# The opening of the first feed-forward layer: smaller first chunks, halved adaLN columns, modulation from PSUM

## The chip, the core and the metric

The kernel runs on one core of one Trainium2 chip. Time is device time in microseconds (us); each kernel is run several times and the median is given. TensorE (PE) multiplies, VectorE (DVE), ScalarE (ACT) and GpSimd (POOL) work on elements, SyncE (SP) issues the DMAs. Each engine works through its own queue in order and waits on semaphores that others raise.

## The reference

One Conformer-like block over 256 tokens of width 2048, with adaLN: nine vectors of 2048 (shift, scale, gate for three parts) come from `silu(c) @ w_ada + b_ada`.

```
def modulate(h, shift, scale):
    return h * (1 + scale[:, None, :]) + shift[:, None, :]
def swiglu(h, w_gu, w_down):
    gu = jnp.einsum('bsd,df->bsf', h, w_gu)
    g, u = jnp.split(gu, 2, axis=-1)
    return jnp.einsum('bsf,fd->bsd', jax.nn.silu(g) * u, w_down)
...
ada = jnp.einsum('bd,de->be', c_act, w_ada[l]) + b_ada[l]
sh1, sc1, g1, shm, scm, gm, sh2, sc2, g2 = jnp.split(ada, N_MOD, axis=-1)
h = modulate(rms_norm(x, ffn1_norm[l]), sh1, sc1)
x = x + FFN_RESIDUAL_WEIGHT * g1[:, None, :] * swiglu(h, ffn1_w_gu[l], ffn1_w_down[l])
h = modulate(rms_norm(x, mix_norm[l]), shm, scm)
x = x + gm[:, None, :] * hybrid_mixer(h, ...)
h = modulate(rms_norm(x, ffn2_norm[l]), sh2, sc2)
x = x + FFN_RESIDUAL_WEIGHT * g2[:, None, :] * swiglu(h, ffn2_w_gu[l], ffn2_w_down[l])
```

The width of the feed-forward layers is 5632; everything is float32.

## The kernel before

Activations stay on the chip; weights stream through once, mostly in tiles of 1 MB: four row tiles of 128 rows by 512 columns. Each tile is split in two parts: ACT rounds it (line 222, a CAST from `raw` to `whi`), DVE takes the exact remainder (line 224, `wlo`). The activations are split in the same way. A product is three passes on PE (lines 232 to 234): high by high, high by low, low by high, for each row tile and each of two tiles of 128 tokens. So a row tile has six matrix instructions, called products here. The token-tile accumulators of a chunk are in PSUM; ACT copies them out (line 345).

An adaLN column of 128 values comes from a tile of `w_ada` of 1 MB: DVE multiplies it by `silu(c)`, which stands on every partition, and sums along the row (line 152). Two columns, scale and shift, modulate one row tile of the activations (128 channels).

The first feed-forward layer has 22 chunks of 256 columns of gate and 256 of up. At its start only few adaLN columns are there, so stage A takes just the first row tiles of a chunk: `EXT` gives 1 for the first three chunks, 2 for three, 3 for five, and 4 for the rest. The rows left out come later: a second stage, A2, takes eight chunks (`n_a2`) through their first rest and second piece, then the chunks are finished one by one. The modulation of the first block of 512 channels is made in tiles: for each of the two token tiles DVE scales and shifts out of PSUM (line 293), ACT rounds (295), DVE subtracts (296).

The order is not written by hand engine by engine: the program is written as one sequence and a tile framework puts it into the engines' queues, by its own estimate of when things are ready. `issue_after` holds a DMA back in that order until another has been issued. Buffers are pools: four raw weight buffers (`raw`), four of `whi` and of `wlo`, 32 blocks of 4 KB per partition (`blk`), six accumulators. A DMA into a pool waits until the buffer's last reader is done. Loads run three tiles ahead (`AHEAD`) of the products.

Of the kernel before, what the change touches and what calls it, by code (L numbers as in the profile page):

```python
# [16 lines left out]
F32 = mybir.dt.float32  # L17
# [30 lines left out]
# columns of the packed small parameters  # L48
# [3 lines left out]
def _cols():  # L52
    pos = 0
    for name, n in (("bada", 144), ("ident", P), ("n1", 16), ("nm", 16), ("n2", 16), ("convw", 8 * CK),
                    ("convb", 8), ("lng", 8), ("lnb", 8), ("subln", 1), ("qn", DH), ("kn", DH), ("lam", 4 * DH),
                    ("inv", 32), ("mask", P)):
        _COLS[name] = (pos, n)
        pos += n
    return pos
# [6 lines left out]
def block_kernel(ctx: ExitStack, tc: tile.TileContext, x_in, c_in, pos_in, w_ada, small, w_gu1, w_dn1,  # L66
# [3 lines left out]
    blkp = ctx.enter_context(tc.tile_pool(name="blkp", bufs=32))  # L70
# [30 lines left out]
    # ---------------------------------------------------------------- constants  # L101
    c_bc = const.tile([P, D], F32, name="c_bc")
    c_row = [blk([1, 1024]) for _ in range(2)]
    ones_r = tmp([1, P])
    nc.gpsimd.memset(ones_r, 1.0)
    for i in range(2):
        nc.sync.dma_start(out=c_row[i], in_=c_in[:, i * 1024:(i + 1) * 1024])
        for j in range(2):
            pc = acc_tile()
            nc.tensor.matmul(pc, ones_r, c_row[i][:, j * 512:(j + 1) * 512], start=True, stop=True)  # L110
            o = (2 * i + j) * 512
            nc.scalar.activation(out=c_bc[:, o:o + 512], in_=pc, func=AF.Silu)
    cst = const.tile([P, NCOLS], F32, name="cst")
    pos_i = const.tile([P, NT], I32, name="pos_i")

# [4 lines left out]
    ident = col("ident")  # L120
    identb = const.tile([P, P], BF16, name="identb")
    maskb = const.tile([P, P], BF16, name="maskb")
    half = const.tile([P, 8], F32, name="half")
    nc.gpsimd.memset(half, -0.5)

    def rstd_of(ss, n, count, eps):
# [16 lines left out]
    # ---------------------------------------------------------------- adaLN projections  # L143
    ada_cols = {}

    def ada(j):
        g = j // 8
        if j % 8 == 0:
            ada_cols[g] = const.tile([P, 8], F32, name=f"ada{g}")
# [8 lines left out]
    ada_next = [0]  # L158
# [18 lines left out]
    def modulation(base, k, norm):  # L177
        """Scale and shift columns of the 128-channel tile k."""
# [9 lines left out]

    def gate(base, scale):
        """The gate's 2048 values on every partition, as four [P, 512] views (through DRAM)."""  # L190
# [37 lines left out]

    def mm3(acc, a, w, start, stop):
# [6 lines left out]
    def mm_tile(accs, w, act, k0, start, stop, ts=(0, 1), ks=(0, 4)):  # L236
        """One weight tile (row tiles ks of the four from k0) into the accumulators of the token tiles."""
# [8 lines left out]
    # ---------------------------------------------------------------- residual stream  # L246
    x = []
# [9 lines left out]
    class Norm:  # L257
        """RMS norm and modulation of the residual stream into split, transposed activations."""
# [13 lines left out]
        def begin(self, kb, t, vec):  # L272
            """Normalised and transposed tokens, still without modulation."""
# [14 lines left out]
        def tile(self, st_, kb, t, j):  # L288
            """One 128-channel tile, modulated and split."""
            tp, hf = st_  # L290
            G, SH = modulation(self.base, 4 * kb + j, self.norm)
            hi = self.hh[kb][:, j, t * P:(t + 1) * P]
# [32 lines left out]
    # ---------------------------------------------------------------- FFN  # L325
    HOLD = 3        # weight tiles held across a change of the activations
    HOLD_DN = 2     # and at the end of a down projection

    def ffn(st, w_gu, w_dn, gate_base, ada_a, ada_b, nxt, n_a2, n_a3):
        """nxt: the norm that follows (None after the last layer).  # L330

        Stage A takes the first row tiles of every chunk.  Then n_a2 chunks get their second piece (the
        last n_a3 of them the third too) ahead of the rest, so that the adaLN columns have time to come.
        """
# [12 lines left out]
        def pieces(after=None):  # L347
            # the last activations take the place that the first leave after stage A
# [6 lines left out]
        begun = 4 * bool(st.done)       # row tiles whose activations are there  # L355
        ext = [4] * NCH                 # row tiles of a chunk in stage A
        if not st.done:
            # the first modulations arrive one 128-channel tile at a time
            sts = [st.begin(0, t, True) for t in range(NT)]
            ws = []  # L360
            for c in range(NCH + AHEAD):
                if c < NCH:
# [583 lines left out]
```

## Time and profile before

| | |
|---|---|
| three runs | 1874.54, 1870.46, 1874.64 us |
| median | 1874.54 us |
| span of the profiled execution, first to last instruction | 1872.4 us |
| the profiled execution's own time | not given apart from its span; the median of the runs is 2.1 us above the span |
| mean granted TensorE clock | 0.995 of full |
| PE, DVE, ACT busy in the span | 98%, 77%, 48% |

A row of the timeline gives an instruction, or several alike that follow each other, with its start, its length, and in brackets how long its engine stood idle before it and what ended that. A matrix instruction is drawn with a modelled end and overlaps the next one, so the distance of two starts is the rate. The clock is given as a share of full: 1.00 is 2.4 GHz and 0.50 is 1.2 GHz.

### The profile page before, as it was taken

What the parts mean: (1) busy time and instruction counts of PE and PEld (TensorE: products, weight loads), DVE (VectorE), ACT (ScalarE), POOL (GpSimd) and SP (SyncE); (2) the same over time, 40 slices, a digit from 0 to 9 for tenths busy, and PEclk for the clock granted to TensorE, in tenths of its full rate; (3) what the DMA queues carried; (4) which work ended last, traced back from release to release, by engine and by line L of the source; (5) the groups of instructions that cost most, each with busy time, mean ns of one, the idle gap of its engine ahead of it and who ended that gap; (6) DMA issues with size and microseconds to landing.
All of it is one profiled execution on the core that took longest, in us unless ns stands there. A gap on an engine that the chain in (4) does not pass through costs nothing.

```text
span 1872.4 us, 21954 instructions
## 1 busy us (share of the span) xinstructions
PE 1838.1 (98%) x8295; PEld 1510.8 (81%) x8295; DVE 1439.3 (77%) x1921; ACT 905.5 (48%) x1363; POOL 30.9 (2%) x34
## 2 busy tenths in 40 slices
PE   6999999999999999999999999999999999999999
PEld 3788888888888888778877788888888888888887
DVE  6779889988888777789999688775877755544443
ACT  4654354444444434454876555654444444433332
POOL 0000000000000000000110100000000000000000
PEclk9999999999999999999999899999999999999999
DMA  8888978888898888646343696895777755555552
GB/s 312 341 315 328 364 272 327 330 326 329 317 345 330 335 340 333 226 170 210 137 158 138 241 344 257 328 355 202 274 285 272 275 197 180 190 215 205 201 212 79
DMA packets 72141, 495.92 MB, mean 265 GB/s; under 512 B 8114, under 2 KB 8290, under 8 KB 14052
## 3 DMA queue, kind: packets, MB, share of 16 engines
q1 hardware_dynamic: 72036, 494.53, 71.5%
q8 instruction: 65, 1.06, 0.2%
q14 instruction: 40, 0.33, 0.1%
HBM read 492.37 MB, written 2.12 MB: 264 GB/s over the span
## 4 chain that ended last, share of the span: by engine, by line
PE 91%; DVE 5%; ACT 2%; issue 1%; DMA 1%; POOL 1%; POOLq 0%; ACTq 0%; DVEq 0%
PE acc L233 29%; PE acc L234 29%; PE acc L232 29%; DVE wlo L224 1%; DVE blk L596 1%; PE tp L426 1%; DMA raw<-in_w_ada_dram 1%; PE acc L677 1%; DVE raw L152 1%; PE tp L285 0%; ACT whi L222 0%; PE acc L110 0%; PE tp L740 0%; POOL rs L129 0%; ACT tmp L632 0%
## 5 line engine op out<-in xcount | busy, mean ns | idle before, releaser
L222 ACT CAST whi<-raw 128x1024 fp32r<-128x1024 f32 (+1 forms) x624 | 645.7, 1042 | 773.1 <-PE acc L234 665.9
L224 DVE TENSOR_TENSOR wlo<-raw,whi 128x1024 fp32r<-128x1024 f32 (+1 forms) x624 | 747.5, 1210 | 349.6 <-ACT whi L222 348.6
L232 PE MATMUL acc<-whi,blk 128*128 128x512 f32 x2464 | 966.2, 394 | 12.2 <-ACT whi L222 6.2
L233 PE MATMUL acc<-wlo,blk 128*128 128x512 f32 x2464 | 965.1, 392 | 3.5 <-DVE wlo L224 3.5
L234 PE MATMUL acc<-whi,blk 128*128 128x512 f32 x2464 | 964.8, 392 | 0.5 <-DVE blk L319 0.5
L232 PEld LDWEIGHTS acc<-whi,blk 128*128 128x128 f32 x2464 | 464.2, 189 | 110.0 <-ACT whi L222 8.3
L233 PEld LDWEIGHTS acc<-wlo,blk 128*128 128x128 f32 x2464 | 464.9, 189 | 101.6 <-DVE wlo L224 6.7
L234 PEld LDWEIGHTS acc<-whi,blk 128*128 128x128 f32 x2464 | 464.8, 189 | 97.3 <-DVE blk L319 0.9
L152 DVE CUSTOM_DVE_ANT_0 raw<-raw,c_bc 128x2048 f32<-128x2048 f32 x144 | 328.9, 2285 | 5.2 <-DMA raw<-in_w_ada_dram 5.2
L596 DVE SCALAR_TENSOR_TENSOR blk<-blk,cst,blk 128x256 f32<-128x256 f32 x240 | 100.9, 483 | 0.0
L345 ACT COPY blk<-acc 128x512 f32<-128x512 f32 x88 | 51.0, 589 | 84.6 <-PE acc L234 81.3
L422 DVE TENSOR_TENSOR blk<-acc,blk 128x512 f32<-128x512 f32 x88 | 56.8, 684 | 0.5 <-PE acc L234 0.5
L233 PE MATMUL acc<-blk,blk 128*128 128x512 f32 x96 | 37.4, 391 | 0.5 <-DVE blk L224 0.5
L232 PE MATMUL acc<-blk,blk 128*128 128x512 f32 x96 | 37.8, 394 | 0.0
L234 PE MATMUL acc<-blk,blk 128*128 128x512 f32 x96 | 37.4, 390 | 0.0
L424 DVE TENSOR_TENSOR blk<-blk 128x256 f32<-128x256 f32 x88 | 34.7, 420 | 0.8 <-ACT blk L423 0.7
L423 ACT ACTIVATE blk<-blk 128x256 f32<-128x256 f32 x88 | 33.3, 409 | 2.6 <-DVE blk L422 1.7
L244 DVE TENSOR_TENSOR blk<-tp,blk 128x512 fp32r<-128x512 f32 x44 | 30.0, 685 | 0.9 <-ACT blk L243 0.8
L224 DVE TENSOR_TENSOR blk<-raw,blk 128x1024 fp32r<-128x1024 f32 x24 | 28.7, 1221 | 0.8 <-ACT blk L222 0.8
L426 PEld LDWEIGHTS tp<-cst,blk 128*128 128x128 f32 x176 | 21.6, 140 | 5.6 <-DVE blk L244 0.3
L243 ACT CAST blk<-tp 128x512 fp32r<-128x512 f32 x44 | 25.3, 581 | 1.6 <-PE tp L426 1.6
L426 PE MATMUL tp<-cst,blk 128*128 128x128 f32 x176 | 26.0, 272 | 0.0
(134 smaller groups left out, 624.1 us busy)
## 6 DMA issues: line engine op xcount, KB each, us to landing
raw<-in_w_gu_dram SPq DMA_DIRECT2D x165, 1024.0 KB, 4.9
raw<-in_w_ada_dram SPq DMA_DIRECT2D x144, 1024.0 KB, 5.7
raw<-in_w_dn_dram SPq DMA_DIRECT2D x88, 1024.0 KB, 4.8
raw<-in_w_in_dram SPq DMA_DIRECT2D x40, 1024.0 KB, 4.8
raw<-in_w_out_dram SPq DMA_DIRECT2D x16, 1024.0 KB, 5.4
raw<-in_w_gu_dram SPq DMA_DIRECT2D x8, 768.0 KB, 7.0
raw<-in_w_gu_dram SPq DMA_DIRECT2D x6, 512.0 KB, 6.6
blk<-gate_line SPq DMA_DIRECT2D x6, 512.0 KB, 6.6
```

The source lines that it names most:

```text
L152: nc.vector.tensor_tensor_reduce(out=raw, in0=raw, in1=c_bc, scale=1.0, scalar=0.0, op0=ALU.mult, op1=ALU.add, accum_out=ada_cols[g][:, j ...
L222: nc.scalar.copy(out=hi[:, :m, :], in_=raw[:, h:h + m, :])
L224: nc.vector.tensor_sub(out=lo[:, :m, :], in0=raw[:, h:h + m, :], in1=hi[:, :m, :].bitcast(F32))
L232: nc.tensor.matmul(acc, ah, wh, start=start, stop=False)
L233: nc.tensor.matmul(acc, ah, wl, start=False, stop=False)
L234: nc.tensor.matmul(acc, al, wh, start=False, stop=stop)
L345: last_part[0] = nc.scalar.copy(out=parts[c][:, t, :], in_=accs[t])
L422: nc.vector.tensor_add(out=p[:, t, :], in0=accs[t], in1=p[:, t, :])
L423: nc.scalar.activation(out=p[:, t, :256], in_=p[:, t, :256], func=AF.Silu)
L424: nc.vector.tensor_mul(out=p[:, t, 256:], in0=p[:, t, :256], in1=p[:, t, 256:])
L426: nc.tensor.transpose(tp[:, i, t * P:(t + 1) * P], p[:, t, 256 + i * P:256 + (i + 1) * P], ident)
L596: nc.vector.scalar_tensor_tensor(out=y, in0=u, scalar=w, in1=y, op0=ALU.mult, op1=ALU.add)
```

## The change

x is loaded as two DMAs, one for each tile of 128 tokens, into one constant tile, and the squares are shared alike by ACT and DVE in both; c comes with the packed small parameters, which are loaded first, and is spread over the partitions by 16 transposes. The first two adaLN columns come as four half loads into blocks, each summed by DVE by itself. The first modulation works on both token tiles at once, 256 columns: ACT makes the rounded high part straight from PSUM, DVE makes the full value from PSUM and then subtracts. `tile` with this form is used by the two later norms as well. Stage A begins with seven chunks of one row tile, four of two and three of three; the single-row loads go into blocks, not raw buffers, and chunks 3 and 4, and 5 and 6, share a load and a rounding. The number of adaLN columns that go with each load is a table for the first twelve loads. `n_a2` is 11 (the last three with the third piece) instead of 8 (the last two). The block pool has 28 instead of 32 buffers, since x no longer lies in it.

```
-EXT = (1,) * 3 + (2,) * 3 + (3,) * 5   # row tiles of the first chunks in stage A
+EXT = (1,) * 7 + (2,) * 4 + (3,) * 3
+LOADS = [(0,), (1,), (2,), (3, 4), (5, 6)] + [(c,) for c in range(7, NCH)]
+FIRST_ADA = (0, 0, 1, 1, 1, 1, 1, 0, 1, 1, 1, 1)
...
-    c_row = [blk([1, 1024]) for _ in range(2)]
...
+    xall = const.tile([P, NT, D], F32, name="xall")
+    nc.sync.dma_start(out=cst[:, :first_cols], in_=small[:, :first_cols])
+    for t in range(NT):
+        nc.sync.dma_start(out=xall[:, t, :], in_=x_in[t * P:(t + 1) * P, :])
...
+    def first_modulation():
...
+        for i in range(2):
+            for h in range(2):
+                wa = blk([P, 1024])
+                hs = slice(1024 * h, 1024 * h + 1024)
+                nc.sync.dma_start(out=wa, in_=w_ada[i, :, hs])
+                nc.vector.tensor_tensor_reduce(out=wa, in0=wa, in1=c_bc[:, hs], scale=1.0, scalar=0.0, op0=ALU.mult,
+                                               op1=ALU.add, accum_out=a[:, 2 * i + h:2 * i + h + 1])
...
+    def w_first(cs):
...
+        n = len(cs)
+        raw = blk([P, 2, 512])
+        w_dma[0] = nc.sync.dma_start(out=raw[:, :n, :], in_=w_gu1[cs[0]:cs[0] + n, 0].rearrange("c p n -> p c n")[:, :, :512])
...
-        def tile(self, st_, kb, t, j):
...
-            nc.vector.tensor_scalar(out=hf[:, j, :], in0=tp[:, j, :], scalar1=G, scalar2=SH, op0=ALU.mult,
-                                    op1=ALU.add)
-            nc.scalar.copy(out=hi, in_=hf[:, j, :])
...
+        def tile(self, src, hf, dst):
...
+            k, ts = dst
+            G, SH = modulation(self.base, k, self.norm)
+            hi = self.hh[k // 4][:, k % 4, ts]
+            nc.scalar.activation(out=hi, in_=src, func=AF.Identity, scale=G, bias=SH)
+            nc.vector.tensor_scalar(out=hf, in0=src, scalar1=G, scalar2=SH, op0=ALU.mult, op1=ALU.add)
+            self.last = nc.vector.tensor_sub(out=self.hl[k // 4][:, k % 4, ts], in0=hf, in1=hi.bitcast(F32))
...
-    ffn(norm1, w_gu1, w_dn1, 32, (0.78, 32), (0.74, 100), norm_m, 8, 2)
+    ffn(norm1, w_gu1, w_dn1, 32, (0.78, 32), (0.74, 100), norm_m, 11, 3)
```

The queue of ACT before, from chunk 3's copies to the rounding of chunk 6. `acc` are accumulators, two of each chunk; `blk` beside them holds the chunk's partial sums; `whi` is the rounded weight tile of chunk 5 (`whi_60`) and of chunk 6 (`whi_67`).

```order
L345 COPY blk_74_306<-acc_72_292 128x512
L345 COPY blk_74_306<-acc_73_293 128x512
L222 CAST whi_60_253<-raw_59_251 128x1024
L345 COPY blk_82_333<-acc_80_319 128x512
L345 COPY blk_82_333<-acc_81_320 128x512
L345 COPY blk_91_364<-acc_89_350 128x512
L345 COPY blk_91_364<-acc_90_351 128x512
L222 CAST whi_67_281<-raw_66_279 128x1024
```

The queue of ACT now, from the copies of chunks 5 and 6 to the rounding of chunk 9: `whi_56`, `whi_64` and `whi_74` are the weights of chunks 7, 8 and 9; L329 is the modulation of the third row tile.

```order
L391 COPY blk_78_327<-acc_76_319 128x512
L391 COPY blk_78_327<-acc_77_320 128x512
L391 COPY blk_81_338<-acc_79_330 128x512
L391 COPY blk_81_338<-acc_80_331 128x512
L248 CAST whi_56_258<-raw_55_256 128x1024
L391 COPY blk_89_370<-acc_87_356 128x512
L391 COPY blk_89_370<-acc_88_357 128x512
L248 CAST whi_64_284<-raw_63_282 128x1024
L329 ACTIVATE blk_16_144<-tp_19_147,ada0_168,scales_121 128x256
L391 COPY blk_98_401<-acc_96_387 128x512
L248 CAST whi_74_315<-raw_73_313 128x1024
```

Before, a rounding stood behind the copies of the chunk ahead of it at chunk 6, with chunks 3 to 5 rounded between earlier copies; now the roundings of chunks 7 and 8 each stand behind all copies of the chunk ahead, and that of chunk 9 behind the first of the two.

The queue of DVE before, from the first adaLN column to the first low part of the activations. `ada0` is the pair of columns, `scales` the scale with the norm's gain, `wlo` the remainders of the first three chunks, `tp` the transposed tokens, one for each token tile.

```order
L152 ISA raw_33_168,ada0_167<-raw_33_168,c_bc_84 128x2048
L152 ISA ada0_167 128x1
L152 ISA raw_34_171,ada0_167<-raw_34_171,c_bc_84 128x2048
L152 ISA ada0_167 128x1
L224 TENSOR_TENSOR wlo_37_186<-raw_35_182,whi_36_184 128x512
L156 TENSOR_TENSOR ada0_167<-ada0_167,cst_103 128x2
L224 TENSOR_TENSOR wlo_40_192<-raw_38_188,whi_39_190 128x512
L184 SCALAR_TENSOR_TENSOR scales_109<-ada0_167,cst_103 128x1
L224 TENSOR_TENSOR wlo_43_198<-raw_41_194,whi_42_196 128x512
L293 TENSOR_SCALAR tmp_28_154<-tp_27_149,scales_109,ada0_167 128x128
L293 TENSOR_SCALAR tmp_32_166<-tp_31_161,scales_109,ada0_167 128x128
L296 TENSOR_TENSOR blk_25_146<-tmp_28_154,blk_24_145 128x128
```

The queue of DVE now, from the scaling of the second token tile (L341) to the first remainder of the weights; `adah` are the sums of the half columns.

```order
L341 TENSOR_SCALAR tmp_23_162<-xall_86,rstd_22_158 128x512
L205 ISA blk_26_173,adah_24_169<-blk_26_173,c_bc_96 128x1024
L205 ISA adah_24_169 128x1
L207 SCALAR_TENSOR_TENSOR ada0_168<-adah_24_169,cst_84 128x1
L205 ISA blk_27_178,adah_24_169<-blk_27_178,c_bc_96 128x1024
L205 ISA adah_24_169 128x1
L211 SCALAR_TENSOR_TENSOR scales_121<-ada0_168,cst_84 128x1
L205 ISA blk_28_181,adah_24_169<-blk_28_181,c_bc_96 128x1024
L205 ISA adah_24_169 128x1
L207 SCALAR_TENSOR_TENSOR ada0_168<-adah_24_169,cst_84 128x1
L330 TENSOR_SCALAR tmp_29_185<-tp_18_146,scales_121,ada0_168 128x256
L331 TENSOR_TENSOR blk_17_145<-tmp_29_185,blk_16_144 128x256
```

The remainders of the first three chunks, which stood between the columns and the modulation, now follow it; the first half column is summed before the second token tile's root is taken, the other three after its scaling. On ACT the modulation L329 stands ahead of the first three roundings.

## Rows read from the trace of the kernel before

**Rows 1.** The page, part 1: the line on PE (busy us, share, instructions).
```profile
PE 1838.1 (98%) x8295; PEld 1510.8 (81%) x8295; DVE 1439.3 (77%) x1921; ACT 905.5 (48%) x1363; POOL 30.9 (2%) x34
```

**Rows 2.** Ten-us stretches from 60 to 480 us: sum of busy us by engine.
```profile
sum 420.00, PE 419.60 PEld 346.62 DVE 367.16 ACT 204.61 POOL 0.00; mean PE 9.99 PEld 8.25 DVE 8.74 ACT 4.87 POOL 0.00
```

**Rows 3.** Timeline of PE: start us, us, instruction, [idle us before it <- what ended it].
```profile
21.79 0.79 PE L232 MATMUL acc<-whi,blk 128*128 128x512 f32 x1 [5.61 <-ACT blk L295]
...
29.35 0.73 PE L232 MATMUL acc<-whi,blk 128*128 128x512 f32 x2 [1.62 <-ACT whi L222]
...
30.89 0.73 PE L232 MATMUL acc<-whi,blk 128*128 128x512 f32 x2 [0.81 <-ACT whi L222]
...
36.79 0.50 PE L233 MATMUL acc<-wlo,blk 128*128 128x512 f32 x1 [0.16 <-DVE wlo L224]
...
41.80 0.84 PE L232 MATMUL acc<-whi,blk 128*128 128x512 f32 x2 [2.41 <-ACT whi L222]
...
43.53 0.79 PE L233 MATMUL acc<-wlo,blk 128*128 128x512 f32 x1 [0.89 <-DVE wlo L224]
...
45.40 0.63 PE L232 MATMUL acc<-whi,blk 128*128 128x512 f32 x1
...
45.83 0.63 PE L233 MATMUL acc<-wlo,blk 128*128 128x512 f32 x1
...
50.97 0.73 PE L232 MATMUL acc<-whi,blk 128*128 128x512 f32 x2 [0.92 <-ACT whi L222]
...
52.23 0.50 PE L233 MATMUL acc<-wlo,blk 128*128 128x512 f32 x1 [0.52 <-DVE wlo L224]
...
56.00 0.39 PE L232 MATMUL acc<-whi,blk 128*128 128x512 f32 x1
...
61.89 0.39 PE L234 MATMUL acc<-whi,blk 128*128 128x512 f32 x1
```

**Rows 4.** Timeline of DVE and ACT in the opening.
```profile
13.67 1.04 DVE L280 TENSOR_SCALAR tmp<-blk,rstd 128x512 f32<-128x512 f32 x2 [0.68 <-POOL rstd L129]
...
21.44 0.62 ACT L295 CAST blk<-tmp 128x128 fp32r<-128x128 f32 x2 [0.74 <-DVE tmp L293]
...
38.73 1.28 ACT L345 COPY blk<-acc 128x512 f32<-128x512 f32 x2 [1.94 <-PE acc L234]
...
40.70 1.04 ACT L222 CAST whi<-raw 128x1024 fp32r<-128x1024 f32 x1 [0.69 <-DMA raw<-in_w_gu_dram]
```

**Rows 5.** Groups by line and shape, 0 to 260 us: busy us, mean ns | idle before.
```profile
L224 DVE TENSOR_TENSOR wlo<-raw,whi 128x1024 fp32r<-128x1024 f32 x76 | 91.4, 1222 | 29.8 <-ACT whi L222 29.3
...
L152 DVE CUSTOM_DVE_ANT_0 raw<-raw,c_bc 128x2048 f32<-128x2048 f32 x33 | 75.3, 2286 | 3.9 <-DMA raw<-in_w_ada_dram 3.9
...
L412 DVE TENSOR_TENSOR blk<-acc,blk 128x512 f32<-128x512 f32 x16 | 10.6, 687 | 2.8 <-PE acc L234 2.8
...
L222 ACT CAST whi<-raw 128x512 fp32r<-128x512 f32 x16 | 9.9, 621 | 17.6 <-DMA raw<-in_w_gu_dram 9.3 <-PE acc L234 8.3
...
L317 ACT ACTIVATE tmp<-tp,ada,scales 128x128 f32<-128x128 f32 x12 | 5.0, 456 | 7.6 <-DVE scales L184 5.6 <-DVE tmp L314 2.0
...
L252 DVE CUSTOM_DVE_ANT_0 tmp<-blk 128x512 f32<-128x512 f32 x4 | 2.8, 692 | 8.6 <-DMA blk<-in_x_dram 6.3 <-PE acc L110 2.0 <-ACT tmp L255 0.4
...
L255 ACT ACTIVATE tmp<-blk 128x512 f32<-128x512 f32 x4 | 2.5, 618 | 0.0
```

**Rows 6.** Two-us stretches: busy us (instructions) by engine, PEclk, DMA share, GB/s.
```profile
2.00:4.00 2.00, 1.69 (x2) 0.83 (x3) 0.00 (x0) 0.01 (x1) 0.00 (x0) 1.00 0.64 140
...
4.00:6.00 2.00, 2.00 (x4) 0.80 (x3) 0.54 (x1) 0.60 (x1) 0.00 (x0) 1.00 1.02 374
...
6.00:8.00 2.00, 2.00 (x4) 0.86 (x3) 0.86 (x4) 0.79 (x2) 0.00 (x0) 1.00 0.86 263
...
8.00:10.00 2.00, 1.48 (x2) 0.00 (x0) 0.39 (x1) 0.89 (x2) 0.00 (x0) 1.00 1.05 405
...
46.00:48.00 2.00, 2.00 (x7) 1.51 (x6) 0.69 (x2) 0.00 (x0) 0.00 (x0) 0.50 0.86 331
```

More of the change, by code (lines that the diff above doesn't have):

```diff
@@ L65, in block_kernel @@
 @with_exitstack
-def block_kernel(ctx: ExitStack, tc: tile.TileContext, x_in, c_in, pos_in, w_ada, small, w_gu1, w_dn1,
+def block_kernel(ctx: ExitStack, tc: tile.TileContext, x_in, pos_in, w_ada, small, w_gu1, w_dn1,
                  w_in, w_out, w_gu2, w_dn2, out):
@@ L99, in tp_tile @@
         return tpp.tile(list(shape), F32, tag="tp", name=nm("tp"))
-    c_bc = const.tile([P, D], F32, name="c_bc")
-    c_row = [blk([1, 1024]) for _ in range(2)]
[L104 to L112, printed above, removed]
     cst = const.tile([P, NCOLS], F32, name="cst")
     pos_i = const.tile([P, NT], I32, name="pos_i")
+    xall = const.tile([P, NT, D], F32, name="xall")
+    x = [xall[:, :, n * 512:(n + 1) * 512] for n in range(4)]
+    first_cols = _COLS["nm"][0]
+    nc.sync.dma_start(out=cst[:, :first_cols], in_=small[:, :first_cols])
+    for t in range(NT):
+        nc.sync.dma_start(out=xall[:, t, :], in_=x_in[t * P:(t + 1) * P, :])
     def col(name):
@@ L120, in block_kernel @@
     ident = col("ident")
+    c_col = const.tile([P, KT], F32, name="c_col")
     identb = const.tile([P, P], BF16, name="identb")
@@ L124, in block_kernel @@
     nc.gpsimd.memset(half, -0.5)
+    nc.scalar.activation(out=c_col, in_=col("c"), func=AF.Silu)
+    c_bc = const.tile([P, D], F32, name="c_bc")
+    for i in range(4):
+        pc = acc_tile()
+        for j in range(4):
+            k = 4 * i + j
+            nc.tensor.transpose(pc[:, j * P:(j + 1) * P], c_col[:, k:k + 1].to_broadcast([P, P]), ident)
+        nc.scalar.copy(out=c_bc[:, i * 512:(i + 1) * 512], in_=pc)
     def rstd_of(ss, n, count, eps):
@@ L147, in ada @@
         g = j // 8
-        if j % 8 == 0:
+        if g not in ada_cols:
             ada_cols[g] = const.tile([P, 8], F32, name=f"ada{g}")
@@ L156, in ada @@
             nc.vector.tensor_add(out=ada_cols[g][:, o:o + 2], in0=ada_cols[g][:, o:o + 2], in1=cst[:, p0:p0 + 2])
-    ada_next = [0]
+    ada_next = [2]
     credit = [0.0]
@@ L227, in w_tile @@
         return lambda j: views[j]
+    def w_first(cs):
+        n = len(cs)
+        raw = blk([P, 2, 512])
+        w_dma[0] = nc.sync.dma_start(out=raw[:, :n, :], in_=w_gu1[cs[0]:cs[0] + n, 0].rearrange("c p n -> p c n")[:, :, :512])
+        hi = whp.tile([P, 2, 512], F32R, tag="whi", name=nm("whi"))
+        lo = wlp.tile([P, 2, 512], F32R, tag="wlo", name=nm("wlo"))
+        nc.scalar.copy(out=hi[:, :n, :], in_=raw[:, :n, :])
+        nc.vector.tensor_sub(out=lo[:, :n, :], in0=raw[:, :n, :], in1=hi[:, :n, :].bitcast(F32))
+        return [lambda j, i=i: (hi[:, i, :], lo[:, i, :]) for i in range(n)]
     def mm3(acc, a, w, start, stop):
@@ L353, in pieces @@
                             st.piece(kb, t)
-        begun = 4 * bool(st.done)
         ext = [4] * NCH
         if not st.done:
[L359 to L362, printed above, removed]
-                    ext[c] = EXT[c] if c < len(EXT) else 4
-                    while begun < ext[c]:
-                        with tc.issue_after(w_dma[0].ins) if c else nullcontext():
-                            ada_until(base + 2 * begun + 2)
-                        for t in range(NT):
-                            st.done.add((0, t))
-                            st.tile(sts[t], 0, t, begun)
-                        begun += 1
-                    ws.append(w_tile(w_gu[c, 0], False, (0, ext[c])))
-                    with tc.issue_after(w_dma[0].ins):
-                        ada_share(ada_a[0] * ext[c] / 4, ada_a[1])
-                if c >= AHEAD:
-                    cc = c - AHEAD
-                    stage_a(cc, ws[cc], [acc_tile() for _ in range(NT)], (0, 1), ext[cc])
+            raws, begun = st.begin_both(), [0]
@@ new lines, in ffn, with load, begin_ready @@
+            ws = {}
+            def load(i):
+                cs = LOADS[i]
+                if ext[cs[0]] == 1:
+                    ws.update(zip(cs, w_first(cs)))
+                else:
+                    ws[cs[0]] = w_tile(w_gu[cs[0], 0], False, (0, ext[cs[0]]))
+            for c in range(NCH):
+                ext[c] = EXT[c] if c < len(EXT) else 4
+            def begin_ready():
+                while begun[0] < 4 and base + 2 * begun[0] + 2 <= ada_next[0]:
+                    st.tile(raws[begun[0]], tmp([P, S]), (begun[0], slice(0, S)))
+                    begun[0] += 1
@@ new lines, in ffn @@
+            first_modulation()
+            begin_ready()
+            for i in range(len(LOADS) + AHEAD):
+                if i < len(LOADS):
+                    load(i)
+                    with tc.issue_after(w_dma[0].ins):
+                        if i < len(FIRST_ADA):
+                            ada_until(ada_next[0] + FIRST_ADA[i])
+                        else:
+                            ada_share(ada_a[0], ada_a[1])
+                        begin_ready()
+                if i >= AHEAD:
+                    cs = LOADS[i - AHEAD]
+                    assert begun[0] >= ext[cs[0]]
+                    for c in cs:
+                        stage_a(c, ws[c], [acc_tile() for _ in range(NT)], (0, 1), ext[c])
```

51 lines of the change are left out of this document (30 added, 21 removed).

## The prediction, made before the changed kernel was run

> **What bounds the kernel now.** First the page's list of engines: TensorE (PE) is busy 98% of the 1872.4 us span [rows 1]. So only what makes PE start earlier, or stop for less time, can move the total; work taken from VectorE (DVE), ScalarE (ACT) or the DMA counts only where PE waits for it. Next the table of ten-us stretches, to see where PE loses time: from 60 to 480 us it is busy 419.60 of 420 us [rows 2]. What is left to win in FFN 1 lies before 60 us. Third the timeline of that opening. The first product with a weight starts at 21.79 us [rows 3]; at 52.23 us the last stop of the opening ends. Between the two the chunks of 1, 1, 1, 2, 2, 2 and 3 row tiles have run, 12 row tiles of 6 products, plus two products of the next chunk: 74. From 56.00 to 61.89 us 26 products start, one per 0.227 us [rows 3]. 74 of those are 16.8 us, so 52.23 - 16.8 = 35.4 us is what the opening costs beyond its products. After it PE does not stop, so the total moves as this figure does.
>
> What it is made of: 21.79 us to the first product; seven stops of 1.62, 0.81, 0.16, 2.41, 0.89, 0.92 and 0.52 us, 7.3 in sum, each really about 0.16 longer because a product is drawn 0.39 us long and issued every 0.227, so 8.5 us; and slow products. The granted clock is 0.50 of full, the lower level of 1.2 GHz, from 46 to 48 us [rows 6], and products start 0.43 us apart there (45.40, 45.83) [rows 3]. The 16 products that this chunk still has at 43.53 us are issued by 50.97 - 0.92 - 0.16 = 49.89 us, in 6.4 us; 16 x 0.227 would be 3.6: 2.7 us more. They follow the longest stop, 2.41 us, and the 0.89 us soon after it. The rest, 2.4 us, is the slow start of the first products and small waits; I leave it equal on both sides.
>
> **Who ends those stops.** The columns name ACT's rounding of a weight tile (the CAST to whi) and DVE's remainder (wlo) [rows 3]. On ACT the row shows why: at 38.73 us it copies the last chunk's two accumulators (1.28 us, 0.64 each) and only then rounds the next weights (1.04 us at 40.70) [rows 4]. ACT works its queue in order, so a CAST that stands behind a copy cannot start before PE has finished the chunk that is copied. I call this a turn and price it from rows. Full turn (both copies ahead of the CAST): the end of the last product 0.16, the second copy 0.64, the CAST 1.04, 0.05 to wake PE: 1.9 us without a product; then two high products (0.45 us) while the remainder takes 1.22 + 0.05 [rows 5], 0.8 us more: 2.7. Half turn (only token tile 0's copy ahead, whose accumulator is ready three products, 0.68 us, sooner): 1.2 + 0.8 = 2.0. The trace has a full turn without its second part (1.62) and a full one with 0.69 us of late data in it (2.41 and 0.89) [rows 3, 4].
>
> **The change, part by part.**
>
> Start. x comes as two loads, the row of c is gone, the small parameters come first. By 8 us the DMA of before had moved 2 x (140 + 374 + 263) GB/s, 1.55 MB, by 10 us 2.4 MB [rows 6]; the new start needs 0.16 + 2.10 MB for both halves of x, so 9 to 9.7 us; I take 9.2. ACT then has two squares of 0.62 us [rows 5]: 10.6. From there DVE runs in order: four half columns, each 0.69 + 512/0.96 ns = 1.22 us (interpolated between the 512-wide 0.69 and the 2048-wide 2.29 [rows 5]) and 0.08 to read the sum, 5.2 in all; between them the second token tile's root, for which DVE waits 0.68, and its scaling, 0.52 [rows 4], and four small operations of 0.2. 10.7 + 5.2 + 1.2 + 0.8 = 17.9. ACT's new modulation of 256 columns from PSUM is 0.456 us [rows 5] and 0.11 for 128 more columns, the first CAST, which stands behind it, 0.62 [rows 5], and each hand-over 0.1 or less: first product at 19.4, 2.4 us earlier than 21.79. Bounds: 17.5 if the root is done beside the column sums and x comes 0.7 us sooner, 20.5 if x is 1 us later.
>
> High part from PSUM. ACT no longer waits for DVE (the 0.74 us ahead of L295 [rows 4] goes), but DVE's own pass, then the remainder and then the weights' first remainder follow ACT's: the first low product finds its operand 0.5 us late. At the two later norms, ACT's step grows from 0.31 to 0.456 us in 8 tiles each, and the DVE step that preceded it goes; between -0.4 and +1.3 us per place, taken as 0.
>
> The order of the chunks. ACT's queue in the new program has copies ahead of the CAST at these places: the pair of chunks 5 and 6 (behind three copies, the last of which is ready 0.68 us before PE ends): 1.6 + 0.4 = 2.0. Chunk 7, behind all four copies of 5 and 6, which ACT works at 0.64 each while PE frees one every 0.45: 2.5 + 0.8 = 3.3. Chunk 8, full: 2.7. Chunk 9, half: 2.0. Chunk 10 stands ahead of its predecessor's copies: 0. Chunks 11 and 12, half: 4.0. Chunk 13: its remainder stands behind a 2.29 us column sum on DVE: 0.9. Chunk 14, full: 2.7. With the 0.5 of the start 18.1 us, against 8.5: +9.6. The reason is that a chunk of one row tile has six products, 1.4 us, for two copies of 0.64 on ACT, and one of two rows 2.7 us for 1.28 of copies and 1.04 of CAST, which is less cover than the three-row chunks that stood at these places. Both ends: if none of the turns had to be paid, -8.5; if each half turn is a full one, +11.7.
>
> Single-row loads through the block pool. They take no raw buffer, so SP can run ahead of DVE; since the CASTs now wait for copies and not for data, the 0.69 us of late data [rows 4] should vanish, which is already in the prices. The Trainium skill says in "DMA: Bandwidth & Descriptors", section Bandwidth, that DMAs should be batched to 1 MiB or more for 75% of the peak, which speaks against loads of a quarter of that.
>
> The slow clock. Before pays one fall, 2.7 us. The new opening has a stop as long (2.5 and 0.8 with two products between) and then four pairs of 1.2 to 1.9 and 0.8. I take one fall again: 0. Bounds: none, -2.7; two more, +5.4. The Trainium skill, "TensorE: Matmul & The Clock Gate", Part 1, says the count of slow matmuls varies from run to run of one kernel. The three runs of before lie 4.2 us apart, which fits a fall that some runs miss; by that rule the sum has an uncertainty of one fall either way, and its middle stays.
>
> Second pieces. n_a2 goes from 8 to 11, three chunks with two additions of 0.687 us more [rows 5]: 4.1 us on DVE, which is busy 367.16 of 420 us while PE runs through [rows 2]: 0. Without that cover +4.1. Six fewer columns fall into FFN 1 and four more into FFN 2, 2.29 us each on DVE; also 0.
>
> Sum: -2.4 + 9.6 = +7.2 us, 1872.4 + 7.2 = 1879.6 us of span. The page gives no time of its own for the profiled execution; the median of the three runs, 1874.54, is 2.1 above the span, so I add 2.1: 1881.7, given as 1882.
>
> **The rivals.** (a) The turns are paid, the forecast: 1878 to 1886, 0.55. (b) Faster: ACT runs ahead. If PE is slower in its first products than I reckon and still has products left when the CASTs of chunks 7, 8 and 9 end, their copies cost nothing, the stops stay at 8.5 and the early start is won: 1874.5 - 2.4 = 1872; such stops bring no fall either, 1869.4; with the earliest start of 17.5, 1867.5. It decides where the stops sum to less than 10.9 us (8.5 + 2.4). For it: SP is freed of raw buffers, and in before one CAST waited for data. Against it: the copies wait for PE, not for data. 0.17. (c) No change: half of the turns are hidden and a fall is missed: +3.5 or less, 1872 to 1878, 0.18. (d) Data late: the small loads keep the queues shallow, and each of the eight turns pays the 0.69 us of [rows 4] on top and a second fall comes: 1881.7 + 5.5 + 2.7 = 1890, 0.10. The rule on batching is about this one; the rate of 374 to 405 GB/s with pieces of 0.5 MB [rows 6] speaks against it.
>
> **How the numbers follow.** Three runs of before scatter by 0.2%, so 0.3%, 5.6 us, is about what can be told from no change. Slower than 1880.2: 0.7 of (a), 0.38, and (d), 0.10: 0.48. Faster than 1868.9: the better two thirds of (b), 0.12. Within: the rest of (a), 0.17, (c), 0.18, and the rest of (b), 0.05: 0.40. The range of 1871 to 1890 leaves about 0.14 below and 0.05 above; the likeliest case's own is 1878 to 1886.
>
> **What would show it.** The first product near 19.4 us; PE stops of about 3.3, 2.7 and 2.0 us in pairs between 30 and 75 us, ended by the CAST of a weight tile and then by the wlo of the same tile; ACT rows in which copies end right where that CAST begins; PE without stops only from about 75 us, not 52; one or two stretches at half clock. Wrong, if CASTs wait for DMA, if the first product is later than 20.5, or if the stops sum to under 11 us.

## The result and the profile after

The changed kernel takes 1879.54 us (median of 7 runs, 1877.68 to 1883.54), the kernel before in the same series 1873.83 (7 runs, 1870.46 to 1875.89): 5.7 us slower, ratio 1.0031, 95% interval 1.002 to 1.0041. The prediction was 1882, range 1871 to 1890. The profiled run of the changed kernel is its slowest one (1883.54 us, span 1881.7), so its trace stands 9.3 us behind the span of before, not 5.7; about 4 us of that is what this run has more than the median, and the parts below say where.

First the engines and the stretch after the opening: the page's PE row and the sum row of the sixty-us stretches from 60 to 480 us.

```profile
PE 1841.0 (98%) x8303; PEld 1511.7 (80%) x8303; DVE 1442.8 (77%) x1924; ACT 908.3 (48%) x1360; POOL 30.8 (2%) x33
```

```profile
sum 420.00, PE 416.95 PEld 343.33 DVE 356.51 ACT 199.42 POOL 0.00; mean PE 59.56 PEld 49.05 DVE 50.93 ACT 28.49 POOL 0.00
```

PE is still the bound. From 60 to 480 us it now stands for 3.05 us where it stood for 0.40 [rows 2]: the opening no longer ends at 52 us. The timeline of PE in the opening, all rows with a stop (idle time before the row and who ended it, in brackets):

```profile
18.16 0.80 PE L269 MATMUL acc<-whi,blk 128*128 128x512 f32 x1 [4.06 <-ACT whi L262]
19.29 0.79 PE L270 MATMUL acc<-wlo,blk 128*128 128x512 f32 x1 [0.34 <-DVE wlo L263]
28.38 1.19 PE L269 MATMUL acc<-whi,blk 128*128 128x512 f32 x4 [1.01 <-ACT whi L262]
33.46 0.73 PE L269 MATMUL acc<-whi,blk 128*128 128x512 f32 x2 [1.71 <-ACT whi L248]
34.72 0.50 PE L270 MATMUL acc<-wlo,blk 128*128 128x512 f32 x1 [0.53 <-DVE wlo L250]
40.26 0.73 PE L269 MATMUL acc<-whi,blk 128*128 128x512 f32 x2 [1.62 <-ACT whi L248]
41.52 0.50 PE L270 MATMUL acc<-wlo,blk 128*128 128x512 f32 x1 [0.53 <-DVE wlo L250]
45.78 0.72 PE L269 MATMUL acc<-whi,blk 128*128 128x512 f32 x2 [0.34 <-ACT whi L248]
47.04 0.50 PE L270 MATMUL acc<-wlo,blk 128*128 128x512 f32 x1 [0.53 <-DVE wlo L250]
53.25 0.73 PE L269 MATMUL acc<-whi,blk 128*128 128x512 f32 x2 [0.94 <-ACT whi L248]
54.51 0.50 PE L270 MATMUL acc<-wlo,blk 128*128 128x512 f32 x1 [0.53 <-DVE wlo L250]
59.37 0.74 PE L269 MATMUL acc<-whi,blk 128*128 128x512 f32 x2 [0.50 <-ACT whi L248]
60.63 0.50 PE L270 MATMUL acc<-wlo,blk 128*128 128x512 f32 x1 [0.52 <-DVE wlo L250]
65.48 0.50 PE L270 MATMUL acc<-wlo,blk 128*128 128x512 f32 x1 [0.48 <-DVE wlo L250]
71.05 0.73 PE L269 MATMUL acc<-whi,blk 128*128 128x512 f32 x2 [1.18 <-ACT whi L248]
72.31 0.50 PE L270 MATMUL acc<-wlo,blk 128*128 128x512 f32 x1 [0.53 <-DVE wlo L250]
```

These answer to the PE rows of before [rows 3]. The first product starts 3.63 us earlier (18.16, not 21.79), and fifteen stops follow in place of seven, most of them in pairs: a rounded weight tile is awaited (whi, ACT), and two products later its remainder (wlo, DVE). Their sum as drawn is 11.3 us, each about 0.16 longer because a product is drawn longer than its distance to the next: 13.7 in place of 8.5. The ACT rows around the second and third pair show what stood ahead of the rounding:

```profile
30.41 2.05 ACT L391 COPY blk<-acc 128x512 f32<-128x512 f32 x4 [1.12 <-PE acc L271]
32.33 1.08 ACT L248 CAST whi<-raw 128x1024 fp32r<-128x1024 f32 x1
37.40 0.59 ACT L391 COPY blk<-acc 128x512 f32<-128x512 f32 x1 [4.00 <-PE acc L271]
38.68 0.59 ACT L391 COPY blk<-acc 128x512 f32<-128x512 f32 x1 [0.69 <-PE acc L271]
39.16 1.05 ACT L248 CAST whi<-raw 128x1024 fp32r<-128x1024 f32 x1
```

Read them with the PE rows: the four copies end at 32.46, the CAST begins at 32.33 and ends at 33.41, PE starts at 33.46. From there ACT stands idle for 4.00 us, because the copy that heads its queue waits for PE; the CAST at 39.16 stood behind that copy and the next, and PE, done with the chunk, then waited for it. None of these rows waits for a DMA.

The granted clock in two-us stretches that touch its falls (columns: stretch, its length, busy time and count by engine, then the share of the full clock, the DMA's share and GB/s); the first two rows are the DMA at the start:

```profile
4.00:6.00 2.00, 2.00 (x12) 2.00 (x11) 0.00 (x0) 0.59 (x1) 0.00 (x0) 1.00 1.00 418
6.00:8.00 2.00, 1.02 (x5) 0.61 (x3) 1.39 (x5) 1.93 (x6) 0.00 (x0) 1.00 0.98 414
...
36.00:38.00 2.00, 2.00 (x6) 1.53 (x5) 1.19 (x4) 0.59 (x1) 0.00 (x0) 0.50 0.97 403
...
44.00:46.00 2.00, 1.66 (x5) 0.84 (x4) 0.71 (x4) 1.80 (x3) 0.00 (x0) 0.55 1.01 409
...
74.00:76.00 2.00, 2.00 (x6) 1.59 (x5) 2.00 (x3) 0.00 (x0) 0.00 (x0) 0.50 0.71 209
```

Three falls to the lower level of 1.2 GHz, each right after a pair of stops, where before had one [rows 6], but a longer one (6.8 us, theirs 3.4 each). At the start the DMA moves 418 and 414 GB/s, where it had moved 374 and 263 [rows 6].

Adding up both traces from the starts of their rows, to the 166th instruction of PE from the first product on (four of them are transposes of tokens before, eight after): before reaches it at 72.61 us, after at 76.49, 3.9 later. Of this the first product is -3.6; stops +5.8 (8.6 and 14.4, each from start to start less 0.227); slow products +1.8 (5.3 and 7.0). The 166th product itself, with the transposes left out of the count, starts at 73.52 and 78.34 us, 4.8 later. Later markers are the reciprocal roots of the norms on POOL, which PE's transposes wait for. The rows for the mixer's norm, of before and then of after:

```profile
766.31 0.55 POOL L129 TENSOR_TENSOR rstd<-rstd,half 128x1 f32<-128x1 f32 x1 [752.12 <-DVE rstd L128]
```

```profile
770.78 0.55 POOL L135 TENSOR_TENSOR rstd<-rstd,half 128x1 f32<-128x1 f32 x1 [758.38 <-DVE rstd L134]
```

So FFN 1 as a whole costs 4.5 us, nearly all of it in its opening. The other 4.8 us of this trace come after 1041 us: 2.2 by the first root of FFN 2's norm (1128.88 us before, 1135.57 after), 2.6 behind it. The waits of PE there that grew or are new:

```profile
1061.80 0.69 PE L803 MATMUL tp<-cst,rv 128*128 128x128 f32 x2 [1.83 <-POOL rv L817]
...
1160.66 0.50 PE L270 MATMUL acc<-wlo,blk 128*128 128x512 f32 x1 [0.74 <-DVE wlo L250]
...
1245.26 0.50 PE L270 MATMUL acc<-wlo,blk 128*128 128x512 f32 x1 [0.91 <-DVE wlo L250]
```

The first was 0.67 us before. From 1041 to 1070 us the granted clock is also lower, 0.76 in place of 0.82. The other two waits are new: remainders of FFN 2's weights that stand on DVE behind adaLN columns, of which 38 in place of 34 are now left for FFN 2. DVE ahead of the second wait (the column is the last of three):

```profile
1157.11 2.28 DVE L158 CUSTOM_DVE_ANT_0 raw<-raw,c_bc 128x2048 f32<-128x2048 f32 x1
...
1159.40 2.35 DVE L250 TENSOR_TENSOR wlo<-raw,whi 128x1024 fp32r<-128x1024 f32 x2
```

### The profile page after: what moved, and what is told of

Its sections match the earlier page's. It is cut to its first block, busy times and chain, and to the rows that moved or that the text cites. A ratio compares the mean times of both kernels' runs of the same rounds, so it can differ in the third digit from the quotient of the medians.

```text
span 1881.7 us, 21957 instructions
## 1 busy us (share of the span) xinstructions
PE 1841.0 (98%) x8303; PEld 1511.7 (80%) x8303; DVE 1442.8 (77%) x1924; ACT 908.3 (48%) x1360; POOL 30.8 (2%) x33
## 4 chain that ended last, share of the span: by engine, by line
PE 89%; DVE 5%; ACT 2%; issue 2%; DMA 1%; POOL 0%; SPq 0%; POOLq 0%; ACTq 0%; DVEq 0%
PE acc L270 29%; PE acc L271 29%; PE acc L269 28%; DVE wlo L250 2%; DVE blk L651 1%; PE tp L486 1%; ACT whi L248 1%; PE acc L732 1%; DVE raw L158 1%; DMA blk<-in_w_ada_dram 0%; PE tp L795 0%; PE tp L320 0%; DMA raw<-in_w_ada_dram 0%; ACT blk L391 0%; POOL rs L135 0%
## 5 line engine op out<-in xcount | busy, mean ns | idle before, releaser
L158 DVE CUSTOM_DVE_ANT_0 raw<-raw,c_bc 128x2048 f32<-128x2048 f32 x142 | 324.2, 2284 | 13.9 <-DMA raw<-in_w_ada_dram 13.7
```

The costliest lines, as they stand in the source:

```text
L158: nc.vector.tensor_tensor_reduce(out=raw, in0=raw, in1=c_bc, scale=1.0, scalar=0.0, op0=ALU.mult, op1=ALU.add, accum_out=ada_cols[g][:, j ...
```

## The experiments

All numbers are medians of the named runs against the kernel before in the same series (1874.43 us of 21 runs for the first four kernels, 1873.86 of 21 for the others). Theory 1 is the turns on ACT; theory 2 the later stages.

**Rounding first.** The decisive one: not an instruction more or less, only the place of the copies in ACT's queue.

```diff
-            for t in ts:
-                last_part[0] = nc.scalar.copy(out=parts[c][:, t, :], in_=accs[t])
+            with tc.issue_after(behind.ins) if behind else nullcontext():
+                for t in ts:
+                    last_part[0] = nc.scalar.copy(out=parts[c][:, t, :], in_=accs[t])
...
+                    behind = casts[i - AHEAD + 1] if ext[cs[0]] < 4 else None
```

> The changed kernel, in which the copies of a chunk's accumulators are queued on ACT behind the rounding of the next weight tile, for the chunks of fewer than four row tiles; nothing else. Theory 1 (the turns): the stops that end with a CAST go (1.01, 1.71, 1.62, 0.34, 0.94, 0.50 and 1.18 us in the profile of the changed kernel, 7.3, each about 0.16 longer than drawn, 8.4), and with them one or two of its three slow stretches (1.3 to 1.9 us each); some stops on wlo stay. 6 to 9 us less than the changed kernel, 1871 to 1874, so no slower than the kernel before. Theory 2 (later places, where adaLN columns moved): the opening is not what costs, 1878 to 1880 as the changed kernel. Theory 3 (the accumulators are the bound: copies that go later hold PE instead): the stops move from the CAST to PSUM and the time stays within 2 us of the changed kernel.

Measured: 1872.44 us (11 runs), ratio 0.9987 (0.9978 to 0.9996), 7.1 us below the changed kernel. The waits of PE from 18 to 140 us (total, times, longest), of this kernel and then of the changed one from 19 us:

```profile
PE acc L271 <- DVE wlo L251: 4.6, 6, 1.2
PE acc L270 <- ACT whi L263: 4.1, 1, 4.1
PE acc L270 <- ACT whi L249: 1.3, 2, 0.9
PE acc L271 <- DVE wlo L264: 0.3, 1, 0.3
```

```profile
PE acc L269 <- ACT whi L248: 6.3, 6, 1.7
PE acc L270 <- DVE wlo L250: 3.6, 7, 0.5
PE acc L269 <- ACT whi L262: 1.0, 1, 1.0
PE acc L270 <- DVE wlo L263: 0.3, 1, 0.3
```

Leaving out the one wait before the first product (4.1), waits for a rounding fall from 7.3 us in seven places to 1.3 in two, and no wait for an accumulator appears: theory 3 falls, theory 1 stands. The 166th instruction starts at 66.89 us in place of 76.49, the mixer's root stands at 761.36 in place of 770.78. The profiled runs lie off their medians (after 4.0 us above, this one 2.4 below), so the medians differ by less than these 9.4 us. The queue of ACT shows the next limit on this road:

```profile
36.20 0.58 ACT L393 COPY blk<-acc 128x512 f32<-128x512 f32 x1
38.81 1.05 ACT L249 CAST whi<-raw 128x1024 fp32r<-128x1024 f32 x1 [2.04 <-DMA raw<-in_w_gu_dram]
```

With the copies out of the way, five roundings between 38 and 62 us wait for their data, 0.76 to 2.83 us, and PE stands 0.39 and 0.88 us for the first two of them; in the opening of the changed kernel none waits for data.

**The old order of chunks.** Everything else of the change is kept.

```diff
-EXT = (1,) * 7 + (2,) * 4 + (3,) * 3
-LOADS = [(0,), (1,), (2,), (3, 4), (5, 6)] + [(c,) for c in range(7, NCH)]
-FIRST_ADA = (0, 0, 1, 1, 1, 1, 1, 0, 1, 1, 1, 1)
+EXT = (1,) * 3 + (2,) * 3 + (3,) * 5
+LOADS = [(c,) for c in range(NCH)]
+FIRST_ADA = (0, 0, 1, 1, 0, 1, 1, 0, 1, 1, 1)
...
-    ffn(norm1, w_gu1, w_dn1, 32, (0.78, 32), (0.74, 100), norm_m, 11, 3)
+    ffn(norm1, w_gu1, w_dn1, 32, (0.78, 32), (0.74, 100), norm_m, 8, 2)
```

> The changed kernel with the row pattern of the kernel before (chunks of 1, 1, 1, 2, 2, 2 and five of 3 row tiles, one load for each chunk, eight chunks with second pieces), and all else of the change: x by token tile, four halves, high part from PSUM, loads of one row through the block pool. Theory 1: it keeps the earlier start (3.6 us, 18.16 against 21.79) and has the stops of the kernel before (8.5 us in place of 13.7): some 5 us below the changed kernel in the opening and one fall of the clock in place of three, together 1871 to 1875. Theory 2: 2 to 4 us of the loss lie behind the opening, so 1874 to 1877. If the order costs nothing: 1879.

Measured: 1872.46 us (11 runs), ratio 0.9992 (0.9983 to 1.0), again 7.1 us below the changed kernel; the first product at 18.14 us, the 166th instruction at 66.88, the mixer's root at 761.94. So the rest of the change, start included, is worth some 2 us, though its start alone is 3.6 earlier.

**The new order alone**, in the kernel before:

```diff
-EXT = (1,) * 3 + (2,) * 3 + (3,) * 5   # row tiles of the first chunks in stage A
+EXT = (1,) * 7 + (2,) * 4 + (3,) * 3   # row tiles of the first chunks in stage A
...
-    ffn(norm1, w_gu1, w_dn1, 32, (0.78, 32), (0.74, 100), norm_m, 8, 2)
+    ffn(norm1, w_gu1, w_dn1, 32, (0.78, 32), (0.74, 100), norm_m, 11, 3)
```

> The kernel before with only the row pattern of the change (chunks of 1 x 7, 2 x 4, 3 x 3 row tiles, one load for each chunk, second pieces of eleven chunks). Theory 1: the start stays at 21.79 us, and the new order of chunks brings the turns on ACT: 4 to 8 us slower than the kernel before, 1878 to 1882. Against it: here every chunk has its own load and the next rounding may stand elsewhere in ACT's queue; if the pairs of single-row chunks make the turns, and not the smaller chunks, it is 1872 to 1876.

Measured: 1881.06 us (5 runs), ratio 1.0038 (1.0025 to 1.0051): 6.6 us slower than before. That is the time forecast, but not its cause. Its trace is not behind in the opening: the 166th product starts at 73.42 us (73.52 before), the 300th at 103.80 (104.43 before). By the 350th it is 7.0 us behind (122.76 and 115.76), by two stops of PE that neither before nor the changed kernel has:

```profile
113.64 1.27 PE L285 MATMUL tp<-cst,tmp 128*128 128x128 f32 x8 [1.30 <-ACT tmp L282]
116.95 1.22 PE L232 MATMUL acc<-whi,blk 128*128 128x512 f32 x2 [2.05 <-ACT whi L222]
```

PE waits for the scaled tokens of the next block and then for a rounding that ACT does between their modulations, and from 115 to 123 us the granted clock is 0.57. So the 6.6 us here and the 7.1 of the run above are not the same loss, and the one does not confirm the other. The row pattern with its second pieces brings only some of the turns here (0.94 and 0.53 us at 52 us and again at 58), and the opening does not lose by them. The run above put back the shared loads and the table of columns as well; which part of the change the other turns need besides the pattern is not shown.

**The columns put back.** More columns in FFN 1, so that the later stages find what they found before.

```diff
-    ffn(norm1, w_gu1, w_dn1, 32, (0.78, 32), (0.74, 100), norm_m, 11, 3)
+    ffn(norm1, w_gu1, w_dn1, 32, (0.78, 32), (0.79, 100), norm_m, 11, 3)
...
+    credit[0] = 0.2
     accs = {}
     def out_tile(n, pc, start, stop, held=False):
```

> The changed kernel with its adaLN columns put back to the places of the kernel before from the mixer on: 0.79 columns per weight tile in FFN 1's later stages in place of 0.74, and the fraction that is owed at the output projection set to 0.2. The opening is as in the changed kernel. Theory 1: the opening is the whole loss, so 1878 to 1880. Theory 2: the profile of the changed kernel stands 4.4 us behind the kernel before at the mixer, and 9.3 at the end; the stops of 0.74 and 0.91 us on wlo in FFN 2's opening and the longer wait for rv (1.83 against 0.67 us) come from columns that now stand ahead there. They go: 2 to 4 us less, 1875.5 to 1877.5.

Measured: 1885.8 to 1887.8 us in five runs, 7 us above the changed kernel where 2 to 4 below were expected. A miss; its one profiled execution ran at half pitch throughout (last section), so the kernel was run again for its trace.

> The kernel of the run with the columns put back, once more, for its trace: that run's profiled execution took 3758.6 us with PE at half pitch throughout and can't be read beside the others, and its five timed ones took 1885.8 to 1887.8, 5 to 8 us more than the changed kernel where 2 to 4 less were expected. Theory 2 as it was (the columns cost only in the later stages) has no place for this. New theory: at 0.79 per tile the columns of FFN 1 are not all done before its end; they stand on DVE ahead of the last additions to the residual and of the mixer's norm, so the root of norm_m (770.78 us in the changed kernel) and PE's stop there come 3 us or more later, and FFN 1 itself loses 1 to 3 us to remainders that stand behind columns. Rival: the loss lies in the opening, which then takes more than in the changed kernel.

Measured: 1884.82 us (one run). Its opening is that of the changed kernel with fewer slow products (166th instruction at 74.36 us), and FFN 2 has no stop on wlo any more, as theory 2 said. At the 3001st instruction it is still 2.7 us ahead of the changed kernel's trace (706.18 and 708.92 us), at the attention's first root 5.4 behind (899.8 and 894.4). Three stops of PE lie between:

```profile
711.44 0.50 PE L270 MATMUL acc<-wlo,blk 128*128 128x512 f32 x1 [0.79 <-DVE wlo L250]
...
773.76 0.63 PE L320 MATMUL tp<-cst,tmp 128*128 128x128 f32 x4 [2.40 <-DVE tmp L315]
...
841.66 0.79 PE L270 MATMUL acc<-wlo,blk 128*128 128x512 f32 x1 [2.65 <-DVE wlo L250]
```

The first is what the new theory said, a remainder late in FFN 1; the changed kernel has no stop there, none at the second place (the mixer's norm), and 1.10 us at the third (837.78 us). On DVE the reason for the second is a change of neighbours, and not a column:

```profile
768.90 0.69 DVE L522 TENSOR_TENSOR tmp<-acc,blk 128x512 f32<-128x512 f32 x1 [5.50 <-PE acc L271]
769.51 1.22 DVE L250 TENSOR_TENSOR wlo<-raw,whi 128x1024 fp32r<-128x1024 f32 x1
770.64 0.69 DVE L523 TENSOR_TENSOR xall<-xall,tmp 128x512 f32<-128x512 f32 x1
```

With other columns around it, the order put a remainder of 1.22 us between the two additions that end FFN 1; the root comes 1.8 us later than in the changed kernel, and PE stops. After the second and the third stop come 13 products at 0.43 us (from 777 us, and from 840 to 850 us, where 0.83 of the clock is granted). At the third stop seven steps of the convolution (2.85 us) stand on DVE ahead of the remainder, where four (1.66 us) do in the changed kernel. 0.79 + 2.40 + 1.55 of stops, 0.4 for their hidden ends, 13 x 0.2 = 2.6 for slow products: 7.7 of the 8.1 us.

**POOL rounds the two-row tiles**, to empty ACT's queue in another way.

```diff
-            nc.scalar.copy(out=hi[:, :m, :], in_=raw[:, h:h + m, :])
+            if n == 2:
+                nc.gpsimd.tensor_copy(out=hi[:, :m, :], in_=raw[:, h:h + m, :])
+            else:
+                nc.scalar.copy(out=hi[:, :m, :], in_=raw[:, h:h + m, :])
```

> The changed kernel in which POOL, not ACT, rounds the weight tiles of two row tiles (chunks 7 to 10 in the opening, and four such second halves later); ACT keeps its copies and all other roundings. Theory 1: for chunks 7 to 10 no rounding stands behind copies any more, so the stops ended by ACT at 33.46, 40.26 and 45.78 us (1.71, 1.62 and 0.34) go, and the one at 53.25 with its queue as it was stays; 3 to 5 us less than the changed kernel, 1874 to 1877, if POOL's rounding of 1024 elements, which no trace here shows, takes no more than about 2.5 us (a chunk of two row tiles is 2.7 us of products). Rival: POOL is slower than that and the stops only change their owner: 1879 or more.

Measured: 1883.39 us (4 runs), ratio 1.0052 (1.0037 to 1.0068): the rival. The stops changed their owner: 2.53, 0.72 and 1.33 us for remainders on DVE and 1.54 for POOL in place of the turns of chunks 7 to 9. POOL's and DVE's rows show a price that was not in the bet:

```profile
28.05 1.04 POOL L249 CAST whi<-raw 128x1024 fp32r<-128x1024 f32 x1 [15.61 <-PE acc L274]
31.79 3.05 POOL L249 CAST whi<-raw 128x1024 fp32r<-128x1024 f32 x1 [2.70 <-DVE blk L334]
```

```profile
31.66 2.28 DVE L158 CUSTOM_DVE_ANT_0 raw<-raw,c_bc 128x2048 f32<-128x2048 f32 x1
...
33.87 2.05 DVE L253 TENSOR_TENSOR wlo<-raw,whi 128x1024 fp32r<-128x1024 f32 x1
```

The second rounding, beside a column sum on DVE, takes three times the first, and the remainder behind the sum 2.05 us in place of 1.23.

**Both cures together**: the old order of chunks and the rounding first.

> The changed kernel with both edits that took time back: the row pattern of the kernel before, and the copies queued behind the rounding of the next weight tile. Theory 1: the two edits take away partly the same stops. The run with the old pattern had 3.0 us of stops ended by a CAST or by copies ahead of it (0.92, 0.27 and 1.18, with two of 0.53 after them), of which about 2 to 3 us are left to win: 1869 to 1871. If the two did not overlap, 7 us each below the changed kernel, it would be 1865; if the old pattern has no turns left to remove, 1872 to 1873.

Measured: 1870.63 us (11 runs), ratio 0.9987 (0.9978 to 0.9996). The 166th instruction starts at 62.59 us, stops from start to start sum to 5.0 us up to there: the time is the one forecast for the overlap. This beats both kernels, 3.2 us below the one before and 8.9 below the changed one.

**And the columns earlier**, 0.82 per tile and 0.2 owed, on top of it.

> The kernel with the old row pattern and the copies behind the rounding, and besides the adaLN columns at 0.82 per tile in FFN 1's later stages (so that they are done before its end), with 0.2 owed at the output projection, so that FFN 2 begins with the columns and the fraction of the kernel before. Theory 2: the stops on wlo in FFN 2's opening (0.7 to 1.7 us in the runs with four columns more there) go: 1 to 2 us less than the same kernel without it. Rival: DVE has no room in FFN 1 for the faster rate, and as many stops appear there: the same or 1 to 3 us more.

Measured: 1870.46 us (11 runs), ratio 0.9985 (0.9976 to 0.9994): the same as without it. FFN 2 has one stop of 0.3 us left from 1100 to 1300 us, in place of 0.3 and 0.7; from the first root of FFN 2's norm to the end it takes 744.2 us in place of 745.5. But the opening and FFN 1 had 1.7 us more of stops in its profile, and the mixer's root stands 3.1 us later. Theory 2's stops are real, but another place takes back what they give.

## Why the prediction was right, by its steps

The forecast, case (a), came out: slower, and by turns on ACT. Taking its terms in turn:

*Start, -2.4: under-priced, -3.6.* The bound of 17.5 was nearer than the value of 19.4. Of that bound's two conditions one was met: x came sooner (the DMA moved 2 x (297 + 418 + 414) GB/s, 2.26 MB, by 8 us, which the sum had by 9.2). The other was not: POOL takes the second token tile's root at 11.85 us, and DVE stands 0.67 us for it, as the sum had it. The rest came from DVE's run of half columns and small operations, 6.5 us (10.47 to 16.94) where the sum had 7.2, and from the way on to PE, 1.2 us where it had 1.5.

*Turns, +9.6: over-priced, +5.2 to +6.3.* Every place was right: stops at chunks 5/6, 7, 8, 9, 11, 12 and 14, in pairs but for 5/6, none at chunk 10, a remainder alone at 13. Reading the parts from start to start, less 0.227 a product, the second part of a pair costs 0.80 (0.11 for the second high product, 0.69 for the low one behind it), as priced, and the full turn of chunk 8 costs 2.8, where 2.7 was forecast. Too large were chunk 7 (2.7, not 3.3), the half turns of chunks 5/6 and 9 (1.5 each, not 2.0) and the remainder of 13 (0.6, not 0.9). At chunks 12 and 14 four transposes, 0.11 us apart, run inside the wait (58.27 and 69.27 us), which leaves 1.5 and 2.2 of 2.0 and 2.7. One price was misread: 0.64 us for a copy is half of the 1.28 in [rows 4], but there the second copy waits for PE and starts 0.70 behind the first. Copies that wait for nothing start 0.48 apart (four in 2.05 us), so ACT's queue runs out sooner; chunk 7, behind four, shows it most. And the 0.8 of a second part contains the late high product, which the 8.5 of before leaves out. Counted alike, the parts sum to 15.3 us in place of 18.1, against some 9.0 before.

*Clock, 0 within -2.7 to +5.4.* Three falls in the profiled run in place of one, but each half as long: some 2 us. How many there are differs between executions of one opening: the second look at the kernel with the columns put back has the same opening and one such stretch, and its slow products after the first 5 us sum to 2.9 us where the changed kernel's sum to 5.7. That can be part of why the profiled run lies 4 us above the median.

*Modulation from PSUM and n_a2, 0: right as far as the markers tell.* From the mixer's root to the last root of the attention's norms (1036.65 and 1041.09 us) both traces take 270.3 us. The edit to the later norms was not run by itself.

*Columns, 0: wrong.* The step said that four more columns in FFN 2 were covered (and six fewer in FFN 1; by the mixer's root 96 are done in place of 100, four fewer). DVE has room on average there, but PE waits for one remainder at a time, and a column of 2.28 us ahead of it is a stop: 0.74 and 0.91 us in the trace after. From the first root of FFN 2's norm to the end before takes 743.6 us and after 746.2. The two other traces with after's 38 columns (the rounding first, and POOL) take 746.0 and 746.4, the two with before's 34 (the second look, and the last kernel) 744.2 each: some 2 us are the price of the columns, and the 0.6 that is left is not explained. Of the 2.2 us just ahead of that root 1.2 are the longer wait for rv, which is still 1.30 us with the columns put back, so they alone do not make it; the lower clock there differs between runs (from 1036 to 1065 us the kernel with the rounding first has 0.94 where before has 0.82).

Sum: -3.6 + 5.8 + 1.8 by the 166th instruction and some 2 in FFN 2, against -2.4 + 9.6 + 0 + 0. The mechanism was right; that the total came so near was in part luck, since the over-priced turns stood in for the slow products and the columns that were left at nothing.

*The rivals.* (b), ACT running ahead, did not happen on its own; the experiment with the rounding first is what it would have looked like. Its 1872.4 falls on the 1872 that was worked out for it, but by other terms: a start 1.2 us better than reckoned, and columns that were left at nothing. (d), data late: no CAST of the opening waits for a DMA after the change.

*What would show it.* First product by 19.4 (18.16), stops in pairs ended by CAST and then wlo, copies that end where the CAST begins: seen. Stops until about 75 us: the last at 72.31. One or two stretches at half clock: three.

## What to carry to other kernels

Where one engine both empties accumulators and prepares the next operand, smaller chunks do not just start earlier: each brings the same number of copies with fewer products to hide them, and in a queue worked in order the preparation waits for the engine that waits for it. Look for idle time of the preparing engine directly ahead of a copy, with the preparation right behind it: the cure is to queue the preparation first, and it was worth 7.1 us here with no instruction changed. Where the preparation lands in the queue decides the cost: the same row pattern in the kernel before lost nothing in its opening. And a background task of 2.3 us on an engine that is busy 77% of the time is not hidden by the rest, if the bound waits for that engine's next instruction.

## What the runs showed of the hardware that was not expected

*POOL and DVE hold each other up.* A rounding of 128x1024 takes POOL 1.04 us by itself, and 3.05 when it begins 0.13 us after a column sum on DVE; it ends 0.90 us after that sum does. The remainder that follows on DVE then takes 2.05 us, where it takes 1.23 elsewhere. The Trainium skill states this in "SBUF — State Buffer", section "Who interferes with whom": a DVE instruction with two SBUF inputs contends with a GpSimd instruction that reads SBUF, over a shared port pair that it calls an exclusive lock. The trace agrees, with these three durations.

*A whole execution at half pitch.* One execution of the kernel with the columns put back took 3758.6 us; its others took 1886 to 1888. Two rows of its PE timeline and a stretch of twenty us:

```profile
1500.29 0.72 PE L269 MATMUL acc<-whi,blk 128*128 128x512 f32 x1
1500.74 0.71 PE L270 MATMUL acc<-wlo,blk 128*128 128x512 f32 x1
```

```profile
1500.00:1520.00 20.00, 20.00 (x45) 1.00 0.41 159
```

45 products in 20 us, 0.44 apart, as at the lower level of 1.2 GHz, while the granted clock is recorded as 1.00 and a column sum on DVE takes its usual 2284 ns. The Trainium skill, "TensorE: Matmul & The Clock Gate", section "Seeing it yourself", warns that the clock's events in a trace have been unreliable; here the pitch of the products told it, and the recorded clock did not. What kept the clock there is not shown.
